# The merge with W_A done inside the gate loop one block behind, the gated convolution kept in SBUF, and the router fed by DMA transposes of the split rows

## The chip, the cores and the metric

The kernel runs on one core of a Trainium2 chip. A time is the device time of one execution in microseconds (us). The kernel before was timed in three runs: 1108.13, 1108.33 and 1110.32 us, so its median is 1108.33 us. A further execution, the profiled one, took 1110.83 us, of which 1109.1 us lie between the first and the last instruction (the span); the other 1.7 us lie around it.

## The reference, cut to what matters

One decoder layer on x of 1024 tokens by 1024 features, all in float32:

```python
h = rms_norm(x, attn_norm_g)
q, k, v, f_logit, cb, cc, cu, ga, gb = split(h @ w_in)
y_att  = forgetting_attention(q, k, v, log_f)              # 1024 x 512
y_conv = cb * causal_short_conv(cc * cu, conv_w)           # 1024 x 512
merged = (sigmoid(ga) * (y_att @ w_out_att)                # W_A
          + sigmoid(gb) * (y_conv @ w_out_conv))           # W_B
x  = x + merged @ w_o
h2 = rms_norm(x, ffn_norm_g)
x  = x + hierarchical_moe(h2, w_rg, b_rg, w_re, b_re, ...) # 4 + 16 router columns
h3 = rms_norm(x, ple_norm_g)
x  = x + sigmoid(h3 @ w_pg) * (p @ w_ple)
```

The change touches the lines from `merged` to the router's logits (h2 @ [w_rg | w_re]).

## The kernel before, in words

**Numbers.** Nearly every large product is made of fp16 pairs. `split` (L108) writes a float32 tile as a high part (ScalarE, L110) and a low part (VectorE, L111); `mm3` (L116 to L119) then does three matmuls for each 128-row piece of the contraction: high by high, high by low, low by high. They add up in a PSUM bank of 128 x 512 float32. There are banks named acc (2), tr (2), s (3) and o (1).

**Stages, in order of time.** (1) Projections and attention, with matmuls of the convolution and of gate_A's logits woven in; the logits go to DRAM (`sga`), the attention result too (`yatt`). (2) The gate loop over eight blocks j of 128 features: for each half of 512 tokens, 24 matmuls of gate_B's logits (`feat_mm`, L542, into acc, weights `wgb`; block 0's are done earlier), a sigmoid on ScalarE (L560), 12 matmuls of y_conv with W_B (tiles bmh and bml, into s, L564) and a product on VectorE (L565). The result `sg` is written to DRAM (`cgb`, L566). (3) The merge loop (`merge_in`, `merge`, L590 to L621): for each block it loads `sga` and `cgb` back, takes the sigmoid, does 12 matmuls for each half with W_A and the attention result (yh, yl, into acc), multiplies on VectorE (L607), adds on GpSimd (L608) and splits the sum into mTh and mTl (L609). The eight pieces of w_o are loaded and split along the way (`wo_in`, L581). (4) out_proj (L652): for each of eight token tiles t and each half h, 24 matmuls of mTh, mTl with w_o, and x added by VectorE (L663). `norm2` (L665) makes the normed rows h2, split into h2s, and writes them to DRAM for the experts. The router of tile t-1 stands between: `x2_t` (L682) transposes the float32 rows on TensorE (L687), `pieces` (L674) cuts them into three bf16 parts on ScalarE, VectorE and GpSimd (L675 to L680), `router_mm` (L691) does 24 matmuls of 60 columns (L700). (5) A window for the last tile whose order is written by hand (L880 on): the last out_proj, the routing, and the first matmuls of the last stage (`ple_mm`, L866). (6) The experts and (7) the last combination.

**What sets the order.** Outside the window a scheduler places the instructions on each engine, from dependences and from tiles coming free; each engine, and each engine's queue of DMA issues, then runs strictly in its order. In the attention part ScalarE and VectorE follow the written order until L559. SyncE (SP) issues the weight loads, L533 (`wpiece`), L569, L584, L595, and the x loads, L629. Pools open and close like a stack; a tile in a space that another tile had waits for the last use there. `wraw` tiles in `cp` and `ep` hold raw float32 weights before the split.

Of the kernel before, what the change touches and what calls it, by code (L numbers as in the profile page):

```python
# [9 lines left out]
F32 = mybir.dt.float32  # L10
# [9 lines left out]
S = 1024  # L20
# [6 lines left out]
C = 176  # L27
EPS = 1e-6
WARM = 64
WOJ = (1, 1, 1, 1, 1, 1, 1, 1)  # L30
WOEP = (1, 4, 7)
EA = 1
WRAW = 10
OVR = 2
NPL = 3
# [27 lines left out]
def trunk_layer(ctx: ExitStack, tc: tile.TileContext, x, wq0, wq, wc, wgb, wga, wA, wB, wo, wr,  # L63
# [5 lines left out]
    def pool(stack, name, bufs=1, **kw):  # L69
        return stack.enter_context(tc.tile_pool(name=name, bufs=bufs, reuse_waits="tile", **kw))  # L70
# [3 lines left out]

    yatt = tc.dram_tile([4, 128, S], F32, name="yatt")
    sga_d = tc.dram_tile([8, 128, S], F32, name="sga")
    cgb_d = tc.dram_tile([8, 128, S], F32, name="cgb")
    h2_d = tc.dram_tile([S, 2 * D], FP16, name="h2d")
    mark_d = tc.dram_tile([1, 1], F32, name="mark")
    pl_d = tc.dram_tile([S, D], F32, name="pld")  # L80
# [52 lines left out]
    def o_bank():  # L133
        return bank("o", 1)
# [390 lines left out]
    cstack = ExitStack()  # L525
    cp = pool(cstack, "conv", side="right")
    pieces = itertools.count()

    def wpiece(src, kn, pl_=None):
        i = next(pieces)  # L530
        pl_, n = (cp, 2) if pl_ is None and i % 2 == 0 else (ep, 2)
        raw = pl_.tile([128, 1024], F32, name="wraw", bufs=2 if pl_ is cp else 1)
        nc.sync.dma_start(raw, src)  # L533
        wh = pl_.tile([128, 1024], FP16, name="wh", bufs=n)
        wl = pl_.tile([128, 1024], FP16, name="wl", bufs=n)
        split(wh, wl, raw, scale=HS)
        return (wh.rearrange("p (k m) -> p k m", k=kn), wl.rearrange("p (k m) -> p k m", k=kn))

    def gt_(n=5):
        return ep.tile([128, S], F32, name="g", bufs=n)  # L540

    def feat_mm(wp, h):  # L542
        acc = acc_bank()
        for k in range(8):
            mm3(acc, wp[0][:, k], wp[1][:, k], hTh[:, k, h * 512:(h + 1) * 512],
                hTl[:, k, h * 512:(h + 1) * 512], k, 8)
        return acc

    wBp = None
    for j in range(8):  # L550
        wb = wpiece(wgb[j], 8) if j else None
        if j % 2 == 0:
            wBp = wpiece(wB[j // 2], 4)
        sg = gt_()
        for h in range(2):
            hs = slice(h * 512, (h + 1) * 512)
            a = feat_mm(wb, h) if j else conv["b", h]
            if j == 0 and h == 1:
                order.close()  # L559
            nc.scalar.activation(sg[:, hs], a, AF.Sigmoid, scale=1.0 / PS)  # L560
            b = bank("s", 3)
            jj = slice((j % 2) * 128, (j % 2 + 1) * 128)
            for k in range(4):
                mm3(b, wBp[0][:, k, jj], wBp[1][:, k, jj], bmh[:, k, hs], bml[:, k, hs], k, 4)  # L564
            nc.vector.scalar_tensor_tensor(sg[:, hs], b, 1.0 / PS, sg[:, hs], op0=ALU.mult, op1=ALU.mult)  # L565
        nc.scalar.dma_start(cgb_d[j], sg)  # L566
    for p in range(4):
        yr = cp.tile([128, 1024], F32, name="wraw", bufs=2)
        nc.sync.dma_start(yr, yatt[p])  # L569
        split(yh[:, p], yl_[:, p], yr, scale=XS)  # L570
    cstack.close()
    hstack.close()

    mstack = ExitStack()
    mp = pool(mstack, "merged")
    mTh = mp.tile([128, 8, S], FP16, name="mTh")
# [1 line left out]
    wp_ = pool(mstack, "wo")  # L578
    wos = []

    def wo_in():  # L581
        k = len(wos)
        raw = wp_.tile([128, D], F32, name="woraw", bufs=1) if k not in WOEP else ep.tile([128, D], F32, name="wraw", bufs=1)
# [6 lines left out]
    def merge_in(j):  # L590
        if j % 2 == 0:
            wAs.append(wpiece(wA[j // 2], 4, ep))
        ga, gb = gt_(), gt_()
        for t, d in ((ga, sga_d), (gb, cgb_d)):
            nc.sync.dma_start(t, d[j])  # L595
        nc.scalar.activation(ga, ga, AF.Sigmoid)
        return ga, gb

    def merge(j, ga, gb):
        wAp = wAs[j // 2]  # L600
        jj = slice((j % 2) * 128, (j % 2 + 1) * 128)
        for h in range(2):
            hs = slice(h * 512, (h + 1) * 512)
            a = acc_bank()
            for k in range(4):
                mm3(a, wAp[0][:, k, jj], wAp[1][:, k, jj], yh[:, k, hs], yl_[:, k, hs], k, 4)
            nc.vector.scalar_tensor_tensor(ga[:, hs], a, 1.0 / PS, ga[:, hs], op0=ALU.mult, op1=ALU.mult)  # L607
            nc.gpsimd.tensor_tensor(ga[:, hs], ga[:, hs], gb[:, hs], op=ALU.add)  # L608
            split(mTh[:, j, hs], mTl[:, j, hs], ga[:, hs], scale=XS)  # L609

    wAs, gs = [], []
    for j in range(EA):
        gs.append(merge_in(j))
    for j in range(8):
        if j + EA < 8:
            gs.append(merge_in(j + EA))
        for _ in range(WOJ[j]):
            wo_in()
        merge(j, *gs[j])
    while len(wos) < 8:  # L620
        wo_in()  # L621
    estack.close()
    ystack.close()

# [40 lines left out]
    def norm2(t):  # L665
        h2 = fp.tile([128, D], F32, name="h2", bufs=1)
        rs = row_norm(fp, x2[:, t], gF, h2)
        hs = fp.tile([128, 2, D], FP16, name="h2s", bufs=2)
        nc.scalar.activation(hs[:, 0], h2, AF.Copy)
        nc.vector.tensor_tensor(hs[:, 1], h2, hs[:, 0], op=ALU.subtract)  # L670
        nc.scalar.dma_start(h2_d[t * 128:(t + 1) * 128, :], hs.rearrange("p a d -> p (a d)"))
        return rs

    def pieces(src, parts, rest, eng, extra):  # L674
        nc.scalar.activation(parts[0], src, AF.Copy)  # L675
# [4 lines left out]
        eng.tensor_tensor(parts[2], rest, parts[1], op=ALU.subtract)  # L680

    def x2_t(t, g, fast=False, extra=None):  # L682
        xT = [fp.tile([128, 512], BF, name=f"x2T{i}", bufs=2) for i in range(3)]
        rest = fp.tile([128, 512], F32, name="rest", bufs=1)
# [163 lines left out]
    tb = bank("s", 3)  # L848
    for t in range(NT - 1):
        out_proj(t, 0)  # L850
        if t:
            xT = [x2_t(t - 1, g) for g in range(2)]
        out_proj(t, 1)
        if t:
            router_mm(t - 1, xT, rs)
        rs = norm2(t)
        if t == 4:
            nc.sync.dma_start(wpl, wple)
            nc.sync.dma_start(pTs[0], pT[:, :, :NPL * 128])
# [31 lines left out]
    tr = tr_bank()
    for c in range(4):
# [523 lines left out]
```

## Time and profile before

| | us |
|---|---|
| median of three runs | 1108.33 |
| the profiled execution | 1110.83 |
| its span | 1109.1 |
| gate loop (first bmh matmul to 574) | 460.8 to 574 |
| merge loop | 574 to 625.2 |
| out_proj with norm and router, tiles 0 to 6 and the first half of 7 | 625.2 to 712 |
| hand-ordered window | 712 to 751 |
| experts and the rest | 751 to 1109 |

Over the span TensorE (PE) is busy 94%, VectorE (DVE) 61%, ScalarE (ACT) 49%, GpSimd (POOL) 23%; the granted TensorE clock is 0.975 of full speed in the mean. The stages can be told apart by their lines: matmuls named `s<-bmh,wh` belong to the gate loop, `acc<-yh,wh` to the merge, `acc<-woh,mTh` to out_proj. A matmul row's start is exact enough for a pitch: matmuls are issued one behind another, and each one's listed duration overlaps with its successor's. So time on PE is counted from start to start.

### The profile page before, as it was taken

To read this page: it belongs to the slowest core of one execution; us is meant where nothing else is said; L and a number is where in the kernel's file an instruction comes from. 1 tells how busy PE (TensorE), PEld (TensorE's weight loads), DVE (VectorE), ACT (ScalarE), POOL (GpSimd) and SP (SyncE) were. 2 spreads that over 40 slices of the span, in tenths; PEclk is the share of its full clock that TensorE was granted. 3 is DMA by queue.
4 is the path that set the end of the run, shared out by engine and by line. 5 is a ranking of instruction groups with operands and counts; after the bars stand their busy time and mean duration, and the time that the engine had idled before them with its cause. 6 is when DMAs were issued, how large, how long until landed. Compare 5 with 4: busy or idle time off the path is not lost. (4 is left out here: it accounts for less than half of the span.)

```text
span 1109.1 us, 18207 instructions
## 1 busy us (share of the span) xinstructions
PE 1042.5 (94%) x6776; PEld 602.0 (54%) x6776; DVE 674.2 (61%) x1441; ACT 538.9 (49%) x1001; POOL 253.1 (23%) x364
## 2 busy tenths in 40 slices
PE   5969999999999999999997999987989999997998
PEld 3634555555555544444443455446757777753454
DVE  4866776676666553222337555764987888855633
ACT  4654555555554552212225334345776777753232
POOL 4653333233322000000014322241211111014300
PEclk8979999999999999999999999988999999999999
DMA  7355778675684752333448531159999999716501
GB/s 237 113 120 139 141 157 181 160 140 138 151 163 116 164 134 79 116 105 123 152 139 285 211 128 57 39 175 364 399 380 333 311 337 316 232 62 229 209 39 57
DMA packets 152543, 197.69 MB, mean 178 GB/s; under 512 B 108162, under 2 KB 111754, under 8 KB 152322
## 3 DMA queue, kind: packets, MB, share of 16 engines
q1 hardware_dynamic: 128194, 117.28, 36.9%
q0 software_dynamic: 15136, 53.42, 15.4%
q10 hardware_dynamic: 9120, 25.78, 6.1%
q8 instruction: 54, 0.88, 0.3%
q14 instruction: 39, 0.32, 0.1%
HBM read 138.69 MB, written 32.59 MB: 154 GB/s over the span
## 5 line engine op out<-in xcount | busy, mean ns | idle before, releaser
L118 PE MATMUL acc<-hTl,fwh 128*128 128x512 f16 x336 | 128.4, 382 | 0.0
L117 PE MATMUL acc<-hTh,fwh 128*128 128x512 f16 x336 | 128.3, 382 | 0.0
L119 PE MATMUL acc<-hTh,fwl 128*128 128x512 f16 x336 | 128.2, 381 | 0.0
L947 DVE SCALAR_TENSOR_TENSOR wl<-wraw,wh 128x1024 f16<-128x1024 f32 x64 | 77.4, 1218 | 21.8 <-ACT wh L942 21.8
L111 DVE SCALAR_TENSOR_TENSOR wl<-wraw,wh 128x1024 f16<-128x1024 f32 x47 | 57.0, 1223 | 54.3 <-ACT wh L110 52.8
L228 PE MATMUL acc<-wqh,hTh 128*128 128x384 f16 (+1 forms) x248 | 82.2, 331 | 6.9 <-ACT hTh L110 3.1
L230 PE MATMUL acc<-wql,hTh 128*128 128x384 f16 (+1 forms) x248 | 81.8, 330 | 1.1 <-DVE wql L111 1.1
L229 PE MATMUL acc<-wqh,hTl 128*128 128x384 f16 (+1 forms) x248 | 81.9, 330 | 0.3 <-DVE hTl L111 0.3
L314 ACT ACTIVATE P<-P,st 128x128 f32<-128x128 f32 (+3 forms) x64 | 49.4, 772 | 60.3 <-DVE st L311 40.1
L110 ACT ACTIVATE wh<-wraw 128x1024 f16<-128x1024 f32 x47 | 49.1, 1054 | 55.9 <-PE acc L118 27.5
L942 ACT ACTIVATE wh<-wraw 128x1024 f16<-128x1024 f32 x64 | 66.8, 1052 | 16.1 <-PE acc L1027 8.5
L306 DVE CUSTOM_DVE_ANT_0 P<-s,base 128x512 f32<-128x512 f32 (+2 forms) x96 | 51.2, 552 | 24.4 <-PE s L305 19.4
L323 DVE SCALAR_TENSOR_TENSOR hl<-P,st,hl 128x128 f16<-128x128 f32 (+3 forms) x64 | 52.9, 841 | 17.3 <-ACT hl L322 17.0
L119 PEld LDWEIGHTS <-fwl 128*128 128x128 f16 x336 | 33.1, 98 | 39.3 <-issue 1.1
L1027 PEld LDWEIGHTS <-wh 128*128 128x128 f16 x512 | 50.5, 99 | 5.3 <-issue 1.7
L322 ACT ACTIVATE hl<-P,st 128x128 f16<-128x128 f32 (+3 forms) x64 | 46.5, 767 | 13.7 <-ACT P L314 8.4
L117 PEld LDWEIGHTS <-fwh 128*128 128x128 f16 x336 | 33.1, 98 | 36.0 <-issue 2.4
L1026 PEld LDWEIGHTS <-wh 128*128 128x128 f16 x512 | 51.1, 100 | 1.8
L1310 PE MATMUL acc<-wh,xl 128*128 128x512 f16 (+1 forms) x136 | 49.9, 367 | 2.3 <-DVE xl L111 2.3
L118 PEld LDWEIGHTS <-fwh 128*128 128x128 f16 x336 | 33.0, 98 | 34.4 <-issue 1.1
L991 POOL DMA_INDIRECT xg<-h2d,toki x16 | 18.1, 1131 | 145.0 <-PE tr L1006 135.7
L1311 PE MATMUL acc<-wl,xh 128*128 128x512 f16 (+1 forms) x136 | 49.9, 367 | 0.0
(323 smaller groups left out, 2642.8 us busy)
## 6 DMA issues: line engine op xcount, KB each, us to landing
wraw<-in_we_dram SPq DMA_DIRECT2D x96, 512.0 KB, 6.9
Yd<-yt ACTq DMA_DIRECT2D x14, 512.0 KB, 7.4
fraw<-in_wc_dram POOLq DMA_DIRECT2D x12, 512.0 KB, 5.2
wraw<-in_wq_dram POOLq DMA_DIRECT2D x24, 192.0 KB, 3.9
P<-in_x_dram SPq DMA_DIRECT2D x8, 512.0 KB, 7.4
fraw<-in_wga_dram POOLq DMA_DIRECT2D x8, 512.0 KB, 4.9
base<-brow POOLq DMA_DIRECT2D x8, 512.0 KB, 4.8
sga<-fg POOLq DMA_DIRECT2D x8, 512.0 KB, 3.1
```

Of the source, the lines that this page charges most:

```text
L111: nc.vector.scalar_tensor_tensor(lo, src, scale, hi, op0=ALU.mult, op1=ALU.subtract)
L117: nc.tensor.matmul(acc, lhsT=whi, rhs=xhi, start=k == 0, stop=False)
L118: nc.tensor.matmul(acc, lhsT=whi, rhs=xlo, start=False, stop=False)
L119: nc.tensor.matmul(acc, lhsT=wlo, rhs=xhi, start=False, stop=k == nk - 1)
L228: nc.tensor.matmul(acc[:, :w], lhsT=hTh[:, k, tok], rhs=wh[:, :w], start=k == 0, stop=False)
L229: nc.tensor.matmul(acc[:, :w], lhsT=hTl[:, k, tok], rhs=wh[:, :w], start=False, stop=False)
L230: nc.tensor.matmul(acc[:, :w], lhsT=hTh[:, k, tok], rhs=wl[:, :w], start=False, stop=k == 7)
L306: nc.vector.tensor_tensor_reduce(out=pt[:, c0:c0 + valid], in0=sb[:, :valid], in1=base[:, c0:c0 + valid], scale=1.0, scalar=-3e38, op0=ALU ...
L323: nc.vector.scalar_tensor_tensor(hl[:, :qt + 1, 1], p3, r, hl[:, :qt + 1, 0], op0=ALU.mult, op1=ALU.subtract)
L942: nc.scalar.activation(wh, raw, AF.Copy, scale=HS)
L947: V_.scalar_tensor_tensor(wl, raw, HS, wh, op0=ALU.mult, op1=ALU.subtract)
L1026: nc.tensor.matmul(a[:, :n], lhsT=wh[:, k], rhs=xT[:, k, 0, :n], start=k == 0, stop=False)
```

## The change

Three things change. First, the merge moves: in round j of one loop over j = 0 to 8 the gate work of block j is done and then the merge of block j-1, into the tr banks. The gated convolution stays in SBUF (`gb`, three buffers), so its eight writes to DRAM and eight reads back are gone; the sum with it is now on VectorE (L590 after) and not on GpSimd. One piece of w_o is loaded and split in each round; `wraw` has three buffers, `wh` and `wl` five. Second, the router of tiles 0 to 6 reads DMA transposes (issued by SP) of the split rows h2s, one transposed tile hT2 of 16 blocks of 128 x 128 for each token tile, and does 8 matmuls of 40 and 8 of 20 columns with a split router weight `wrp`; the last tile keeps the old way. Third, since pools open and close at other places, the tiles hTh, hTl are held until after the window, and the loads of gF, the router weights and pT stand behind the x loads.

```diff
-    cgb_d = tc.dram_tile([8, 128, S], F32, name="cgb")
...
-    for j in range(8):
-        wb = wpiece(wgb[j], 8) if j else None
...
-            nc.vector.scalar_tensor_tensor(sg[:, hs], b, 1.0 / PS, sg[:, hs], op0=ALU.mult, op1=ALU.mult)
-        nc.scalar.dma_start(cgb_d[j], sg)
-    for p in range(4):
-        yr = cp.tile([128, 1024], F32, name="wraw", bufs=2)
-        nc.sync.dma_start(yr, yatt[p])
-        split(yh[:, p], yl_[:, p], yr, scale=XS)
-    cstack.close()
-    hstack.close()
...
+    def half_mm(a, wp, xh, xl, jj, hs):
+        for k in range(4):
+            mm3(a, wp[0][:, k, jj], wp[1][:, k, jj], xh[:, k, hs], xl[:, k, hs], k, 4)
+    gB, wAB = {}, {}
+    for j in range(9):
+        if j < 8:
+            wb = wpiece(wgb[j], 8) if j else None
+            if j % 2 == 0:
+                wAB[j // 2] = [wpiece(wB[j // 2], 4)]
+            sg = gB[j] = ep.tile([128, S], F32, name="gb", bufs=3)
+            for h in range(2):
...
+                nc.scalar.activation(sg[:, hs], a, AF.Sigmoid, scale=1.0 / PS)
+                b = bank("s", 3)
+                half_mm(b, wAB[j // 2][0], bmh, bml, slice((j % 2) * 128, (j % 2 + 1) * 128), hs)
+                nc.vector.scalar_tensor_tensor(sg[:, hs], b, 1.0 / PS, sg[:, hs], op0=ALU.mult, op1=ALU.mult)
+            if j == 0:
+                for p in range(4):
+                    yr = ep.tile([128, 1024], F32, name="wraw", bufs=3)
+                    nc.sync.dma_start(yr, yatt[p])
+                    split(yh[:, p], yl_[:, p], yr, scale=XS)
+            if j % 2 == 0:
+                wAB[j // 2].append(wpiece(wA[j // 2], 4))
             wo_in()
+            ga = ep.tile([128, S], F32, name="ga", bufs=3)
+            nc.sync.dma_start(ga, sga_d[j])
+            nc.scalar.activation(ga, ga, AF.Sigmoid)
+            gB[j] = (gB[j], ga)
+        if j:
+            i = j - 1
+            gb, ga = gB.pop(i)
+            for h in range(2):
+                hs = slice(h * 512, (h + 1) * 512)
+                a = tr_bank()
+                half_mm(a, wAB[i // 2][1], yh, yl_, slice((i % 2) * 128, (i % 2 + 1) * 128), hs)
+                nc.vector.scalar_tensor_tensor(ga[:, hs], a, 1.0 / PS, ga[:, hs], op0=ALU.mult, op1=ALU.mult)
+                nc.vector.tensor_tensor(ga[:, hs], ga[:, hs], gb[:, hs], op=ALU.add)
+                split(mTh[:, i, hs], mTl[:, i, hs], ga[:, hs], scale=XS)
...
+    split(wrp[:, :, 0], wrp[:, :, 1], wrt, scale=HS)
...
-        return rs
+        hT2 = fp.tile([128, 2, 8, 128], FP16, name="hT2", bufs=2)
+        nc.sync.dma_start_transpose(hT2.rearrange("p a k t -> p (a k) t"), hs.rearrange("p a d -> p (a d)"))
+        return hT2
+    def router_rows(t, hT2):
+        rb = o_bank()
+        for k in range(8):
+            nc.tensor.matmul(rb[:, :40], lhsT=hT2[:, 0, k], rhs=wrp[:, k].rearrange("p a e -> p (a e)"), start=k == 0,
+                             stop=False)
+            nc.tensor.matmul(rb[:, :20], lhsT=hT2[:, 1, k], rhs=wrp[:, k, 0], start=False, stop=k == 7)
...
         out_proj(t, 0)
-        if t:
-            xT = [x2_t(t - 1, g) for g in range(2)]
         out_proj(t, 1)
         if t:
-            router_mm(t - 1, xT, rs)
-        rs = norm2(t)
+            router_rows(t - 1, hT2)
+        hT2 = norm2(t)
...
     out_proj(T, 0)
-    xT = [x2_t(T - 1, g) for g in range(2)]
...
-    out_proj(T, 1, lambda: router_mm(T - 1, xT, rs))
+    out_proj(T, 1)
...
+    router_rows(T - 1, hT2)
     router_mm(T, last, ss[:, 3:4])
...
+    hstack.close()
```

The first place is SP's queue from the end of attention on; wgb, wB, wA and wo name the four weights, yatt the attention result. Before:

```order
L324 DMA_TRANSPOSE pTr<-hl 128x16x128
L533 DMA wraw<-in_wB_dram 128x1024
L533 DMA wraw<-in_wgb_dram 128x1024 x3
L533 DMA wraw<-in_wB_dram 128x1024 x2
L533 DMA wraw<-in_wgb_dram 128x1024 x4
L569 DMA wraw<-yatt 128x1024
L533 DMA wraw<-in_wB_dram 128x1024
L569 DMA wraw<-yatt 128x1024 x3
L533 DMA wraw<-in_wA_dram 128x1024 x2
L595 DMA g<-sga 128x1024
L595 DMA g<-cgb 128x1024
```

After:

```order
L530 DMA wraw<-in_wB_dram 128x1024
L573 DMA wraw<-yatt 128x1024 x2
L539 DMA woraw<-in_wo_dram 128x1024
L579 DMA ga<-sga 128x1024 x3
L573 DMA wraw<-yatt 128x1024 x2
L530 DMA wraw<-in_wA_dram 128x1024
L539 DMA woraw<-in_wo_dram 128x1024
L530 DMA wraw<-in_wgb_dram 128x1024 x2
L530 DMA wraw<-in_wB_dram 128x1024
```

The attention result and W_A's first piece, which stood behind all gate weights, now stand ahead of the first two of them.

The second place is VectorE in the merge of one block; g (before) and ga (after) hold the gate and then the sum. Before, in the merge loop:

```order
L607 SCALAR_TENSOR_TENSOR g<-acc,g 128x512
L111 SCALAR_TENSOR_TENSOR mTl<-g,mTh 128x512
L111 SCALAR_TENSOR_TENSOR wol<-woraw,woh 128x1024
L607 SCALAR_TENSOR_TENSOR g<-acc,g 128x512
L111 SCALAR_TENSOR_TENSOR mTl<-g,mTh 128x512
L111 SCALAR_TENSOR_TENSOR wl<-wraw,wh 128x1024
```

After, in the joint loop:

```order
L107 SCALAR_TENSOR_TENSOR wl<-wraw,wh 128x1024
L589 SCALAR_TENSOR_TENSOR ga<-tr,ga 128x512
L590 TENSOR_TENSOR ga<-ga,gb 128x512
L107 SCALAR_TENSOR_TENSOR mTl<-ga,mTh 128x512
L589 SCALAR_TENSOR_TENSOR ga<-tr,ga 128x512
L590 TENSOR_TENSOR ga<-ga,gb 128x512
L107 SCALAR_TENSOR_TENSOR mTl<-ga,mTh 128x512
L569 SCALAR_TENSOR_TENSOR gb<-s,gb 128x512
L107 SCALAR_TENSOR_TENSOR wl<-wraw,wh 128x1024
L569 SCALAR_TENSOR_TENSOR gb<-s,gb 128x512
```

The add has come to VectorE, and the products of the gate loop (L569) stand among those of the merge.

The third place is TensorE in out_proj, where the router's operand is made or used. Before, between the halves of a tile:

```order
L662 LDWEIGHTS mTh
L662 MATMUL acc<-wol,mTh 128x512
L687 MATMUL tr<-identF,x_6012 128x128 x8
L660 LDWEIGHTS mTh
L660 MATMUL acc<-woh,mTh 128x512
```

After, the first router matmuls (hT_6125 is tile 0's hT2):

```order
L634 LDWEIGHTS mTh
L634 MATMUL acc<-wol,mTh 128x512
L651 LDWEIGHTS hT_6125
L651 MATMUL o<-wrp,hT_6125 128x40
L653 LDWEIGHTS hT_6125
L653 MATMUL o<-wrp,hT_6125 128x20
L651 LDWEIGHTS hT_6125
```

The transposes are gone from TensorE. Tile 0's router stands 99 matmuls of out_proj behind tile 0's own last one; those of tiles 1 to 5 stand 72, 59, 60, 59 and 72 behind theirs, and tile 6's stands in the window behind the last tile's transposes.

The fourth place is SP behind the merge, where hT2's transposes are issued. Before, the loads of gF, wrt and part of pT stood in the row behind the first place; after:

```order
L599 DMA x_5982<-in_x_dram 128x1024 x8
L610 DMA gF<-in_gains_dram 128x1024
L616 DMA wrt<-in_wr_dram 128x160
```

They stand behind the eight x loads now, and wple, pT and the seven transposes (L645) follow them.

## Rows read from the trace of the kernel before

**Rows 1.** Windows by stage: busy us of each engine (count), clock, DMA share, GB/s.

```profile
461.00:574.00 113.00, 113.00 (x525) 51.22 (x524) 29.94 (x32) 25.51 (x32) 1.51 (x11) 1.00 0.39 133
574.00:625.00 51.00, 44.76 (x196) 19.36 (x194) 39.42 (x48) 25.44 (x31) 21.20 (x15) 0.97 0.70 237
625.00:712.00 87.00, 87.00 (x566) 44.94 (x565) 50.52 (x117) 32.68 (x64) 19.88 (x21) 1.00 0.27 105
712.00:724.00 12.00, 9.66 (x67) 5.02 (x64) 9.18 (x38) 4.12 (x9) 3.54 (x3) 0.86 0.11 45
...
751.00:1006.00 255.00, 235.25 (x2364) 179.09 (x2362) 194.15 (x309) 172.27 (x251) 36.57 (x62) 0.99 0.85 299
```

**Rows 2.** Waits of TensorE, 440 to 760: total us, times, longest.

```profile
PE acc L117 <- DVE g L607: 6.2, 6, 2.2
...
PE s L117 <- ACT wh L110: 1.6, 1, 1.6
```

**Rows 3.** Timeline of TensorE, four starts: start us, us, engine, line.

```profile
460.78 0.39 PE L117 MATMUL s<-bmh,wh 128*128 128x512 f16 x1 [1.63 <-ACT wh L110]
...
533.31 0.38 PE L117 MATMUL s<-bmh,wh 128*128 128x512 f16 x1
...
564.39 0.38 PE L117 MATMUL s<-bmh,wh 128*128 128x512 f16 x1
...
625.24 0.38 PE L660 MATMUL acc<-woh,mTh 128*128 128x512 f16 x1
```

**Rows 4.** Timeline of GpSimd and of VectorE in the merge loop.

```profile
582.31 1.79 POOL L608 TENSOR_TENSOR g<-g 128x512 f32<-128x512 f32 x1 [2.67 <-DVE g L607]
...
582.94 2.25 DVE L111 SCALAR_TENSOR_TENSOR wol<-wraw,woh 128x1024 f16<-128x1024 f32 x1
585.11 0.68 DVE L607 SCALAR_TENSOR_TENSOR g<-acc,g 128x512 f32<-128x512 f32 x1
...
591.64 1.23 DVE L111 SCALAR_TENSOR_TENSOR wl<-wraw,wh 128x1024 f16<-128x1024 f32 x1 [1.57 <-ACT wh L110]
```

**Rows 5.** Groups of TensorE by shape, 440 to 760: busy us, mean ns, idle.

```profile
L700 PE MATMUL o<-wrb,x2T 128*128 128x60 bf16 x180 | 9.4, 193 | 0.0
L687 PE MATMUL tr<-identF,x 128*128 128x128 f32 x60 | 7.9, 274 | 2.3 <-DVE rest L676 2.3
```

**Rows 6.** Timeline of TensorE in out_proj and in the window.

```profile
640.78 1.04 PE L687 MATMUL tr<-identF,x 128*128 128x128 f32 x8
641.65 0.38 PE L660 MATMUL acc<-woh,mTh 128*128 128x512 f16 x1
...
715.92 0.66 PE L687 MATMUL tr<-identF,x 128*128 128x128 f32 x4 [2.34 <-DVE rest L676]
...
720.04 0.38 PE L660 MATMUL acc<-woh,mTh 128*128 128x512 f16 x1
...
721.45 0.77 PE L700 MATMUL o<-wrb,x2T 128*128 128x60 bf16 x22
722.06 0.38 PE L660 MATMUL acc<-woh,mTh 128*128 128x512 f16 x1
```

**Rows 7.** Timeline, norm of token tile 0: from x's second half to h2s.

```profile
635.80 0.69 DVE L663 SCALAR_TENSOR_TENSOR x<-acc,x 128x512 f32<-128x512 f32 x1 [3.62 <-PE acc L662]
...
641.98 0.33 ACTq L671 DMA_DIRECT2D h2d<-h2s  x1
```

**Rows 8.** Line L324, the DMA transposes of attention: landing.

```profile
DMA to landing us min/median/max: 2.3/3.8/4.8
```

**Rows 9.** Line L252, the transposes of the projections: landing.

```profile
DMA to landing us min/median/max: 2.7/2.8/6.0
```

**Rows 10.** Line L629, the x loads: issues and landing.

```profile
L629 SPq DMA_DIRECT2D x<-in_x_dram x8: 333/435/557, 627.5 to 630.9; - x8
...
DMA to landing us min/median/max: 3.6/6.8/11.1
```

**Rows 11.** Line L569, the loads of the attention result: landing.

```profile
DMA to landing us min/median/max: 3.3/3.3/3.4
```

More of the change, by code (lines that the diff above doesn't have):

```diff
@@ L29 @@
 WARM = 64
-WOJ = (1, 1, 1, 1, 1, 1, 1, 1)
-WOEP = (1, 4, 7)
-EA = 1
 WRAW = 10
@@ L524, in trunk_layer @@
     ep = pool(estack, "ep", side="right")
[L525 to L549, printed above, removed]
-    for j in range(8):
-        wb = wpiece(wgb[j], 8) if j else None
[L552 to L564, printed above, removed]
-            nc.vector.scalar_tensor_tensor(sg[:, hs], b, 1.0 / PS, sg[:, hs], op0=ALU.mult, op1=ALU.mult)
-        nc.scalar.dma_start(cgb_d[j], sg)
-    for p in range(4):
-        yr = cp.tile([128, 1024], F32, name="wraw", bufs=2)
-        nc.sync.dma_start(yr, yatt[p])
-        split(yh[:, p], yl_[:, p], yr, scale=XS)
-    cstack.close()
-    hstack.close()
     mstack = ExitStack()
@@ L579, in trunk_layer, with wpiece @@
     wos = []
+    def wpiece(src, kn):
+        raw = ep.tile([128, 1024], F32, name="wraw", bufs=3)
+        nc.sync.dma_start(raw, src)
+        wh = ep.tile([128, 1024], FP16, name="wh", bufs=5)
+        wl = ep.tile([128, 1024], FP16, name="wl", bufs=5)
+        split(wh, wl, raw, scale=HS)
+        return (wh.rearrange("p (k m) -> p k m", k=kn), wl.rearrange("p (k m) -> p k m", k=kn))
     def wo_in():
         k = len(wos)
-        raw = wp_.tile([128, D], F32, name="woraw", bufs=1) if k not in WOEP else ep.tile([128, D], F32, name="wraw", bufs=1)
+        raw = wp_.tile([128, D], F32, name="woraw", bufs=1)
         nc.sync.dma_start(raw, wo[:, k, :])
@@ L588, in wo_in @@
         wos.append((wh, wl))
[L590 to L617, printed above, removed]
-            wo_in()
-        merge(j, *gs[j])
-    while len(wos) < 8:
-        wo_in()
+    def half_mm(a, wp, xh, xl, jj, hs):
[11 more added lines that the diff above has]
+                if j:
+                    a = acc_bank()
+                    for k in range(8):
+                        mm3(a, wb[0][:, k], wb[1][:, k], hTh[:, k, hs], hTl[:, k, hs], k, 8)
+                else:
+                    a = conv["b", h]
+                if j == 0 and h == 1:
+                    order.close()
+                nc.scalar.activation(sg[:, hs], a, AF.Sigmoid, scale=1.0 / PS)
[9 more added lines that the diff above has]
+                wAB[j // 2].append(wpiece(wA[j // 2], 4))
+            wo_in()
+            ga = ep.tile([128, S], F32, name="ga", bufs=3)
+            nc.sync.dma_start(ga, sga_d[j])
+            nc.scalar.activation(ga, ga, AF.Sigmoid)
+            gB[j] = (gB[j], ga)
+        if j:
+            i = j - 1
+            gb, ga = gB.pop(i)
+            for h in range(2):
+                hs = slice(h * 512, (h + 1) * 512)
+                a = tr_bank()
[3 more added lines that the diff above has]
+                split(mTh[:, i, hs], mTl[:, i, hs], ga[:, hs], scale=XS)
@@ L644, in trunk_layer @@
     wrb = fp.tile([128, 8, 60], BF, name="wrb")
+    wrp = fp.tile([128, 8, 2, 20], FP16, name="wrp")
     nc.sync.dma_start(wrt, wr)
+    split(wrp[:, :, 0], wrp[:, :, 1], wrt, scale=HS)
     nc.vector.tensor_tensor(wrt, wrt, vt[:, 40:48, None].to_broadcast([128, 8, 20]), op=ALU.mult)
@@ L671, in norm2 @@
         nc.scalar.dma_start(h2_d[t * 128:(t + 1) * 128, :], hs.rearrange("p a d -> p (a d)"))
-        return rs
+        hT2 = fp.tile([128, 2, 8, 128], FP16, name="hT2", bufs=2)
[3 more added lines that the diff above has]
+        rb = o_bank()
+        for k in range(8):
+            nc.tensor.matmul(rb[:, :40], lhsT=hT2[:, 0, k], rhs=wrp[:, k].rearrange("p a e -> p (a e)"), start=k == 0,
+                             stop=False)
+            nc.tensor.matmul(rb[:, :20], lhsT=hT2[:, 1, k], rhs=wrp[:, k, 0], start=False, stop=k == 7)
+        sm = fp.tile([128, 20], F32, name="sm", bufs=2)
+        nc.vector.tensor_reduce(sm, rb[:, :40].rearrange("p (w e) -> p e w", e=20), axis=AX.X, op=ALU.add)
+        nc.vector.scalar_tensor_tensor(lg[:, t], sm, 1.0 / PS, vt[:, 14:34], op0=ALU.mult, op1=ALU.add)
     def pieces(src, parts, rest, eng, extra):
@@ L682, in x2_t @@
     def x2_t(t, g, fast=False, extra=None):
-        xT = [fp.tile([128, 512], BF, name=f"x2T{i}", bufs=2) for i in range(3)]
-        rest = fp.tile([128, 512], F32, name="rest", bufs=1)
+        xT = [fp.tile([128, 512], BF, name=f"x2T{i}", bufs=1) for i in range(3)]
+        rest = fp.tile([128, 1024], F32, name="hT2", bufs=2)[:, :512]
         tr = tr_bank()
```

## The prediction

> **What bounds the kernel now.** I read the windows by stage first: TensorE is busy all 113 us of the gate loop and all 87 us of out_proj at full granted clock, while VectorE is busy 30 and 51 us there [rows 1]. In the merge loop it is busy 44.8 of 51 us, and there VectorE (39.4 us) and the DMA engines (share 0.70) are loaded most [rows 1]. So TensorE's own instruction stream sets the time, but for the places where it waits. The waits of TensorE between 440 and 760 us name them: 6.2 us, in six pieces, on the product of the merge (VectorE L607), which must free an acc bank, and 1.6 us at the start of the gate loop [rows 2]; the groups by shape give 2.3 us before the router's transposes [rows 5]. I then put a price on the streams, from start to start on the timeline. Between 533.31 and 564.39 us lie two gate blocks without a wait, 144 matmuls in 31.08 us, so 0.2158 us each [rows 3]. From the first bmh matmul, 460.78, to the first of out_proj, 625.24, are 164.46 us [rows 3]; the stream there holds 336 gate_B matmuls (blocks 1 to 7), 192 with W_B and 192 with W_A, 720 x 0.2158 = 155.4 us. 9.1 us are in excess: the 6.2 us of waits, and 2.9 us in which PE ran at half clock (0.97 in the merge window, 1.5 us of 51 [rows 1]) or refilled.
>
> Why VectorE was late: the low part of a w_o piece took 2.25 us with GpSimd's add beside it, and a weight of the same size 1.23 us without [rows 4]. The add itself took 1.79 us, and the next wait stands behind it.
>
> **The change part by part.**
>
> *Gate and merge.* The 720 matmuls remain. In the joint loop a round has 48 + 24 + 24 = 96 matmuls, 20.7 us. VectorE's work in a round: two products of the gate loop, two of the merge and two low parts, of 0.68 us like the old merge's row of that shape [rows 4]; three low parts of weights (wgb, w_o, and half of wB and of wA each) at 1.23 us [rows 4]; two adds that the trace doesn't show on VectorE. GpSimd's 1.79 us [rows 4] bounds one above, zero below; 0.7 us is taken, the 1.23 us row being for twice the elements. That makes 6 x 0.68 + 3 x 1.23 + 1.4 = 9.2 us (11.4 with 1.79) in 20.7, where in the merge loop it was 39.4 of 51. GpSimd has no add left, so the 2.25 us row should go back to 1.23. The merge has the tr banks to itself, so the acc banks wait for ScalarE's sigmoid only. Of the 6.2 us of waits I expect nothing to stay, of the other 2.9 us 1.5. Term: 9.1 - 1.5 = -7.6 us; bounds: 0 (all turns into other waits) and -9.1. The 16 transfers of 512 KB that go were hidden and are worth nothing by themselves.
>
> *Start of the joint loop, an added wait.* TensorE does the 48 bmh matmuls of blocks 0 and 1 first (10.4 us, to 471.1), then the merge of block 0, which needs the attention result and W_A's first piece. These loads stand behind three `sga` loads on SP and wait for a `wraw` tile, so for a split. A load of this kind landed in 3.3 us [rows 11], its low part takes 1.23 [rows 4], and two such turns pass: they end about at 471. The matmuls of gate block 1 are queued behind. Cost 0 to 3.3 (one turn more); taken 0.5, as two turns fit.
>
> *out_proj.* A tile before cost 48 x 0.2158 = 10.36, 8 transposes at (641.65 - 640.78)/8 = 0.109 us, and 24 router matmuls at (722.06 - 721.45)/22 = 0.028 us [rows 6]: 11.9 us. Of the 60 transposes [rows 5] 56 go: -6.1 us. Of the 180 router matmuls [rows 5] 168 go and 112 come; a new one has the same weight load of 128 x 128 and fewer columns, so 0.028 is taken for it (0.02 to 0.04 as ends): -4.7 + 3.1 = -1.6 us (-2.5 to -0.2). The piece-making on ScalarE, VectorE and GpSimd goes too, but they were not what ended last, so that is worth nothing but slack.
>
> *The transposed operand, an added wait at each tile.* Behind out_proj(t,1)'s end come the add to x, the norm and the split: 641.98 - 635.80 = 6.2 us [rows 7]; then SP issues the transpose. The old trace has no transpose of h2s, but attention's largest ones, 16 blocks of 128 x 128 fp16 as well, are among those that landed in 2.3 to 4.8 us [rows 8], and other ones took up to 6.0 [rows 9]. I take 4.8: 6.2 + 4.8 and half a microsecond of hand-over make 11.5 us. The router's 16 matmuls stand at least 59 matmuls of out_proj behind, 12.7 us. Slack 1.2 us; queued behind the waiting matmul is the whole of out_proj, so any lack is paid in full by the end. With 6.0 the lack is 0 too. Taken 0.3 us in all; ends 0 and 7.7 (1.1 us in each tile).
>
> *x, gF.* The x loads wait for the end of the merge, as before; they were issued from 627.5 to 630.9, the last landing up to 11.1 us later, so 14.5 us after the first issue [rows 10]. The first add needs x one transfer (3.6 us) after: 0.3 us taken, up to 2. gF comes behind these eight loads now, and VectorE's scaling of gF stands in its order ahead of the norm and of the last add of tile 1. If M is the last merge matmul, x is issued at M + 3.5, gF lands at about M + 19, and the add of tile 1 ends at M + 22.7. TensorE wants that bank after 36 + 48 + 24 matmuls, M + 23.3. Margin 0.6 us; taken 0.4, up to 4 with a slower landing.
>
> *Window.* The stall of 2.3 us before the transposes [rows 5] goes with them. After it TensorE ran at half clock: from 715.92 to 720.04 it did 4 transposes and 10 matmuls, 4.12 us for 4 x 0.109 + 10 x 0.2158 = 2.59, so 1.5 us lost [rows 6]; the window's 0.86 says the same [rows 1]. What is late next is the add to x before the last transposes, which was late before. Of 3.8 us I take -3.0; ends -3.8 and 0. The experts behind start from this window and have TensorE busy 235 of 255 us [rows 1]; they are taken to shift as a whole.
>
> *Sum.* -7.6 - 6.1 - 1.6 - 3.0 + 0.5 + 0.3 + 0.3 + 0.4 = -16.8 us. The durations are of the profiled execution, 1110.83 us, so it would be 1094.0; that execution was 2.5 us above the median of the runs, and on the median 1108.33 it is 1091.5 us.
>
> **A rule that speaks against it.** The largest transposes of this size landed in at most 4.8 us [rows 8]. The Trainium skill, "VectorE: DVE Perf Modes", sections "The three transpose paths" and "Rules for kernel authors", advises TensorE for a 128 x 128 transpose where PSUM will do as a target, and prices the DMA crossbar at 1309 ns against 390 ns. Sixteen blocks one after another would by that page make an estimated 20.9 us, the router would come some 15 us late in each tile, and the time would go to about 1195 us. The trace disagrees with such a serial sum, with its 4.8 us for 16 blocks.
>
> **The rivals.**
> A. The operand is a little late in every tile: transposes share the DMA engines with 4 MB of x, gF, wple and pT at the beginning, and TensorE loses 1.1 us in each of 7 tiles. For it: the slack is only 1.2 us. Against: out_proj's DMA share was 0.27 [rows 1]. 1091.5 + 7.7 = 1099.2 us. Chance 0.11.
> B. The joint loop starves: SP's order puts the first two pieces of wgb behind eleven other transfers, and each load waits for a `wraw` tile. For it: the merge loop had a DMA share of 0.70 [rows 1]. Against: the round of 20.7 us now moves some 2 MB, 100 GB/s, and the old gate loop moved 133 with no wait. The merge's gain is lost: 1091.5 + 7.6 = 1099.1. Chance 0.06.
> C. Slower: the transposes of h2s land much later than attention's. TensorE's orders are strict, so each microsecond beyond 12.7 - 6.7 = 6.0 us is paid in each of 7 tiles. The point from which it decides is 16.8 / 7 = 2.4 us above this, a landing of 8.4 us; with 10 us the time is 1091.5 + 7 x 4.0 = 1119.5. The rule above is of this kind. For it: the longest transposes seen, 4.8 and 6.0 us, came under light traffic, and SP has other loads queued ahead. Against: none reached 8.4 [rows 8, 9]. Chance 0.05.
> D. The time before the experts is not TensorE's: routing of the last tile, and the experts' loads (DMA share 0.85 [rows 1]) set the end, and what is won above is waited for in the window. 1106 to 1109 us. Against: the last tile's routing begins from TensorE's last out_proj, and the experts' first loads stand on SP behind the last tile's rows, so both begin earlier with it. Chance 0.05.
> E. All terms at their better ends: -9.1 - 6.1 - 2.5 - 3.8 = -21.5, about 1087. Chance 0.03.
>
> **How the numbers follow.** My forecast, 1091.5 us, has 0.70, with its own range 1087.5 to 1095.5 from the ends of the waits and of the window. The range that should hold 8 in 10 takes in E, A and B: 1086.5 to 1099.5. A measurement of this kernel tells about 0.2%, 2.2 us, from no change. Faster by more: forecast, A, B and E, 0.90. Within: D but for a fifth of it, 0.04. Slower: C and that fifth, 0.06.
>
> **What would show it.** In the new trace: from the first bmh matmul to the last of the merge about 157 us instead of 164.5, no wait of TensorE on a product of the merge, no w_o low part above 1.3 us; at the 471st microsecond a pause of under 1 us; a tile of out_proj every 10.8 us instead of 11.9, no weight load of hT2 that waits, and one that landed in 4 to 5 us; no half-clock row about the last tile. The first expert matmul comes some 17 us earlier. The forecast is wrong if TensorE waits for hT2 or gF for more than 3 us in all, if the joint loop has waits for weights, or if the expert stage is longer than before by what was won.

## The result, and the profile after

The changed kernel took 1095.32 us in the median of four runs (1092.79 to 1097.78) against 1108.95 us for the kernel before, measured with it: a ratio of 0.9876, 95% interval 0.985 to 0.9902, so 13.7 us or 1.2% less. Run again later it gave 1092.47 against 1112.94 us for before beside it, 0.9821 (0.9795 to 0.9846). The forecast of 1091.5 us and its range, 1086.5 to 1099.5, hold; the first measurement lies 3.8 us above the forecast.

The profiled execution took 1095.96 us with a span of 1094.2: 14.9 us less than before's span. The windows by stage of the changed kernel, cut at the events of the table below and without the experts (columns as in [rows 1]):

```profile
459.50:618.00 158.50, 158.18 (x732) 71.37 (x733) 71.78 (x88) 51.84 (x64) 1.52 (x11) 1.00 0.31 102
618.00:706.50 88.50, 85.67 (x490) 40.46 (x488) 49.27 (x140) 22.04 (x45) 5.24 (x8) 0.98 0.58 162
706.50:731.00 24.50, 21.13 (x109) 11.27 (x110) 18.76 (x82) 11.26 (x19) 11.21 (x11) 0.93 0.68 227
987.70:1094.20 106.50, 98.00 (x480) 49.91 (x480) 50.30 (x80) 30.84 (x67) 24.17 (x26) 0.95 0.36 129
```

In the first row TensorE (PE) is busy 158.2 of 158.5 us; in [rows 1] the merge part had 44.8 of 51. In the last row the clock is 0.95.

Its waits of TensorE, 440 to 760 us, beside [rows 2]:

```profile
PE tr L989 <- DMA xtail<-h2d,toki: 3.3, 1, 3.3
PE tr L989 <- ACT xT L994: 2.3, 1, 2.3
PE o L651 <- DMA hT<-h2s: 2.1, 1, 2.1
PE s L742 <- DVE oh L740: 2.0, 4, 1.4
PE s L113 <- ACT wh L106: 1.6, 1, 1.6
PE tr L874 <- DVE x L635: 0.7, 1, 0.7
PE o L684 <- DVE sm L655: 0.7, 1, 0.7
PE tr L989 <- DMA xg<-h2d,toki: 0.5, 1, 0.5
...
PE tr L115 <- DVE wl L107: 0.2, 1, 0.2
```

Two rows of the same list for the kernel before, which [rows 2] leaves out:

```profile
PE tr L893 <- DVE x L663: 3.0, 1, 3.0
...
PE s L758 <- DVE oh L756: 0.4, 2, 0.2
```

The 6.2 us on the merge's product are gone, and up to the merge's end only 0.2 us on a weight's low part (L115) have come in their place. New are 2.1 us on the transposed tile (L651); the wait on VectorE's routing (L742, before L758) has grown from 0.4 to 2.0 us; the wait on the add to x ahead of the last transposes (L874, before L893) has fallen from 3.0 to 0.7 us. The first two rows, 3.3 and 2.3 us, stand in the experts, of which this window holds 29 us here and 9.5 us before.

For every kernel I cut the span at five events on TensorE: first bmh matmul; end of the merge (the 12 out_proj matmuls that the new order puts ahead of that end are counted to the next leg); first transpose of the last half tile; first expert matmul; first transposes of the last stage. Here are the cuts of the changed kernel, from its timeline; [rows 3] has two of those of before, and its others are at 727.71, 750.50 and 1007.02 us.

```profile
459.52 0.39 PE L113 MATMUL s<-bmh,wh 128*128 128x512 f16 x1 [1.63 <-ACT wh L106]
...
618.17 0.38 PE L632 MATMUL acc<-woh,mTh 128*128 128x512 f16 x1
...
706.50 0.66 PE L874 MATMUL tr<-identF,x 128*128 128x128 f32 x4 [0.74 <-DVE x L635]
...
730.98 0.24 PE L1009 MATMUL acc<-xT,wh 128*128 128x176 f16 x1
...
987.69 1.49 PE L152 MATMUL tr<-identF,x 128*128 128x128 f32 x8 [3.04 <-DVEq L1218]
```

| leg, us | before | changed | again | merge alone | router alone |
|---|---|---|---|---|---|
| gate and merge | 164.5 | 156.1 | 156.8 | 156.7 | 162.5 |
| out_proj, router | 102.5 | 90.9 | 89.4 | 102.5 | 88.5 |
| window to first expert | 22.8 | 24.5 | 25.3 | 23.2 | 25.2 |
| experts | 256.5 | 256.7 | 255.5 | 259.5 | 255.4 |
| last stage | 102.1 | 106.5 | 104.5 | 102.4 | 101.7 |

So -8.4 and -11.5 us were won, 1.7 given back in the window and 4.4 in the last stage; the first bmh matmul, behind code that is the same, came 1.3 us earlier by itself. The sum is the 14.9 us of the span.

Where most of the 4.4 us went shows on the timeline of TensorE in the last stage of the changed kernel:

```profile
1016.18 0.38 PE L1292 MATMUL acc<-wh,xh 128*128 128x512 f16 x1
1020.44 0.61 PE L1293 MATMUL acc<-wh,xl 128*128 128x512 f16 x1 [3.88 <-DVE xl L107]
1020.84 0.63 PE L1294 MATMUL acc<-wl,xh 128*128 128x512 f16 x1
1021.26 0.63 PE L1292 MATMUL acc<-wh,xh 128*128 128x512 f16 x1
```

Behind a wait of 3.9 us the matmuls run 0.43 us from start to start, half the clock, until 1025.7: 13 of them, 2.6 us lost. In the kernel before the wait is 1.6 us shorter and the clock stays:

```profile
1037.99 0.39 PE L1310 MATMUL acc<-wh,xl 128*128 128x512 f16 x1 [2.27 <-DVE xl L111]
1038.22 0.38 PE L1311 MATMUL acc<-wl,xh 128*128 128x512 f16 x1
```

### The profile page after: what moved, and what is told of

Its sections match the earlier page's. It is cut to its first block, busy times and chain, and to the rows that moved or that the text cites. A ratio compares the mean times of both kernels' runs of the same rounds, so it can differ in the third digit from the quotient of the medians.

```text
span 1094.2 us, 17874 instructions
## 1 busy us (share of the span) xinstructions
PE 1035.9 (95%) x6664; PEld 596.5 (55%) x6664; DVE 667.3 (61%) x1444; ACT 525.4 (48%) x974; POOL 213.7 (20%) x334
## 5 line engine op out<-in xcount | busy, mean ns | idle before, releaser
L115 PE MATMUL acc<-hTh,fwl 128*128 128x512 f16 x336 | 127.3, 379 | 0.0
L302 DVE CUSTOM_DVE_ANT_0 P<-s,base 128x512 f32<-128x512 f32 (+2 forms) x96 | 51.3, 553 | 24.5 <-PE s L301 19.3
L319 DVE SCALAR_TENSOR_TENSOR hl<-P,st,hl 128x128 f16<-128x128 f32 (+3 forms) x64 | 53.0, 842 | 16.8 <-ACT hl L318 16.5
L115 PEld LDWEIGHTS <-fwl 128*128 128x128 f16 x336 | 32.9, 98 | 38.7
L1292 PE MATMUL acc<-wh,xh 128*128 128x512 f16 (+1 forms) x136 | 50.9, 374 | 0.0
```

The costliest lines, as they stand in the source:

```text
L1292: nc.tensor.matmul(a, lhsT=xh[:, k], rhs=wh[:, hs], start=k == 0, stop=False)
```

## The experiments

All but e4 (one round) were timed in five rounds; ratios are to the kernel before on the same chip.

**a0, the changed kernel again**, with no edit.

> The changed kernel once more, for its spread and its clock. Theory: its executions differ only by half-clock stretches of TensorE, so span times granted clock is about 1066.5 us in each (1091.1 x 0.978, 1092.9 x 0.976, 1094.2 x 0.975 gave 1067.1, 1066.7, 1066.8), and the time lies between 1092 and 1098 us, ratio 0.985 to 0.990. In this profile the wait before the last stage's matmuls (low part of x, 3.9 us in the first profile) need not be followed by ten matmuls at half clock. Rival: the give-back in the last stage is part of the change, then every profile has it: 4 to 5 us more than before from the first expert matmul to the end.

Measured: 1092.47 us (1089.59 to 1094.41), ratio as above, lower than expected; span times clock 1063.9 to 1069.7, not as constant as I wrote. The last stage had the wait (3.1 us) and the half clock once more (104.5 us). Of the 14 profiles, the last stage took 101.7 to 102.7 us in before, e1, e2, e4, e5, e7 and e10, and 104.0 to 106.6 in the changed kernel and a0, e3, e6, e8, e9, e11. So a longer last stage goes with most versions that have both parts, but not with all. The rival as written does not hold: from the first expert matmul to the end a0 took 360.0 us and before 358.6, 1.4 us more and not 4 to 5; the first profile took 363.2, e10 353.9, and e1 and e7, with one part or none, 361.9 and 361.2. The wait in the last stage was 1.6 to 2.8 us in the former group and 2.3 to 3.9 in the latter, so the wait alone does not decide it. What does is open.

**e1, the merge alone.**

```diff
-            router_rows(t - 1, hT2)
-        hT2 = norm2(t)
+            router_mm(t - 1, xT, rs)      # with x2_t between the halves, as before
+        rs = norm2(t)
```

> Only the joint loop; the router as before. Theory: the loop's gain (excess 9.1 us before, 0.7 in the changed kernel) stands alone: 8.4 us less, about 1100.5 us, and the window keeps its 2.3 us wait before the router's transposes and the half-clock piece behind it. Rival: the loop's gain depends on the router part (out_proj bound elsewhere): less than 3 us, 1106 or more.

Measured: 1105.42 us, 0.9948 (0.9929 to 0.9966), 5.8 us, less than the 8.4 expected, which lie outside the interval; the rival's 3 us are outside it too. The first leg is 156.7 us, 7.8 less than before, as the theory has it; the 2.3 us wait before the router's transposes (2.4) and a half-clock piece behind it are still there. The experts' leg was 2.9 us longer in this profile, and over the 14 profiles it lies between 251.9 and 259.5 us, so a few us of a gain can be hidden there.

**e2, the router alone**: the loops of before, with norm2, router_rows and the window of the change.

> Only the router by DMA transposes; gate and merge loops as before. Theory: from the first out_proj matmul to the transposes of the last half tile 11.5 us were won, 1.7 given back behind it: about 10 us less, 1099 us; the merge's waits of 6.2 us stay. Rival: the two parts overlap, and this one alone is worth less than 6 us, 1103 or more.

Measured: 1099.66 us, 0.9898 (0.9872 to 0.9924), 11.3 us. Two rows of its waits:

```profile
PE acc L117 <- DVE g L607: 5.8, 7, 1.2
PE s L117 <- ACT wh L110: 1.6, 1, 1.6
```

The merge's waits stay at 5.8 us. The parts add, as far as the noise tells: 5.8 + 11.3 = 17.1 us, and 19.9 for the whole on the same chip in the same rounds, each of the three with an error of 2 to 3 us. The old loops took 162.5 us here, 2 less than before's own profile, whose merge had a piece at half clock; so some 2 of the 8.4 us depend on the execution.

**e3, the write of the rows behind the transpose.**

```diff
-        nc.scalar.dma_start(h2_d[t * 128:(t + 1) * 128, :], ...)   # ahead of the transpose
+        nc.sync.dma_start(h2_d[t * 128:(t + 1) * 128, :], ...)     # behind it
```

> The changed kernel with the write of the normed rows to DRAM issued behind their transpose, on SP, and not beside it on ScalarE's queue. In the changed kernel the transposed tile came 6.3 to 6.6 us after its issue (640.90 to 647.15, 691.32 to 697.92) where attention's took 4.8 at most. Theory: the write of the same rows at the same moment takes the DMA engines; with it behind, the tile comes in at most 5.2 us, the wait of 2.1 us for tile 5's operand falls under 0.8, and the time falls by 1 to 3.5 us against the changed kernel. Rival: the transposes of 16 blocks of this layout take 6.3 us by themselves; nothing changes, within 1 us.

Measured: 1092.11 us, 0.9821, the same as a0. The line of the transposes, first of e2 (write beside it), then of e3:

```profile
L675 SPq DMA_TRANSPOSE hT<-h2s x7: 1687/3958/4391, 642.9 to 709.6; - x7
...
DMA to landing us min/median/max: 5.6/6.0/6.4
```

```profile
L644 SPq DMA_TRANSPOSE hT<-h2s x7: 1317/1935/2892, 643.2 to 700.0; - x7
...
DMA to landing us min/median/max: 4.3/4.7/4.9
```

With the write behind it the transpose of 16 blocks lands in 4.7 us, near the longest of attention's [rows 8]; beside a 512 KB write of the same rows in 6.0. The edit moves the write to another queue as well as behind, so that the two share the DMA engines is the likely reason and not shown by itself. TensorE's wait on the tile fell from 2.1 to 0.3 us and out_proj's leg to 87.9 us, 1.5 to 3 less. The window's grew to 26.0, and the time did not move: the write's effect on the landing is shown, the expected gain in time is not.

**e4, each transpose twice into the same tile.**

> The changed kernel with each DMA transpose issued twice into the same tile, the second behind the first, so that the operand comes about 12 us after the first issue and not about 6. TensorE's order places the router some 15 matmuls (3 us) later. Theory: the operand is on TensorE's path, the distance is about 16 us and 6.7 + 12 are needed: 2 to 3 us lost in each of seven tiles, 1105 to 1115 us, and waits of TensorE on the transposed tile of 12 us or more in all. Rival: the operand has slack enough; within 4 us of the changed kernel.

Measured: 1104.77 us, 0.9931 (0.9912 to 0.995), just under the range given, some 12 us more than a0 by the ratios. TensorE waited 7.4 us in five pieces, not 12:

```profile
PE o L652 <- DMA hT<-h2s: 7.4, 5, 2.3
```

The out_proj leg grew to 98.0 us, and the wait on the last add to x is back at 3.0 us. The operand is on TensorE's path, but TensorE waits less for it than I gave.

**e5, the split rows transposed by TensorE.**

```diff
-        nc.sync.dma_start_transpose(hT2..., hs...)
+        for a in range(2):
+            tr = tr_bank().bitcast(FP16)
+            for c in range(8):
+                nc.tensor.transpose(tr[:, c * 128:(c + 1) * 128], hs[:, a, c * 128:(c + 1) * 128], identH)
+            # copied out by ScalarE (a = 0) and VectorE (a = 1)
```

> The changed kernel with the same split rows transposed by TensorE (16 fp16 transposes of 128 x 128 in a token tile, 0.056 us each by the rows of the experts' transposes) and copied out of PSUM by ScalarE and VectorE. Theory: 7 x 16 x 0.056 = 6.2 us more on TensorE, minus the 2 us wait and 1 us of half clock that the DMA way has: 2 to 5 us slower than the changed kernel. Rival, the rule that prefers TensorE for 128 x 128 blocks: not slower, since no operand comes late any more.

Measured: 1100.23 us, 0.99 (0.9875 to 0.9925), some 8.8 us more than a0 by the ratios; I had expected 2 to 5. Its timeline of TensorE:

```profile
643.25 1.06 PE L651 MATMUL tr<-identH,h2s 128*128 128x128 f16 x16
644.14 0.38 PE L632 MATMUL acc<-woh,mTh 128*128 128x512 f16 x1
...
706.03 0.61 PE L651 MATMUL tr<-identH,h2s 128*128 128x128 f16 x8 [2.03 <-DVE hT L671]
```

16 transposes take 0.89 us, 6.2 in seven tiles, as expected; the wait for the operand is not gone but has become one of 2.0 us for a PSUM bank (VectorE's copy is late), and eight matmuls at half clock follow it. So here, on the kernel's busiest engine and with the copies out of PSUM that the router's operand needs, transposing on TensorE costs time, and 16 blocks by DMA landed in 4.7 us (e3). The Trainium skill ("VectorE: DVE Perf Modes", "Rules for kernel authors") advises TensorE for a 128 x 128 block where PSUM will do as a target; the 20.9 us estimated from the page's 1309 ns did not come.

**e6, the add back on GpSimd in the joint loop** (`nc.vector.tensor_tensor` to `nc.gpsimd.tensor_tensor`, L590).

> The changed kernel with the merge's add on GpSimd as before. Theory: the gain of the joint loop comes from spreading the merge's VectorE work over 20.7 us of matmuls; low parts of weights beside an add stretch to about 2.3 us, but the leg from the first bmh matmul to the end of the merge stays at 156 to 158 us and the time within 1.5 us of the changed kernel. Rival: the gain comes from taking GpSimd off; the leg grows by more than 3 us.

Measured: 1093.56 us, 0.9842 (0.9819 to 0.9866). A low part beside an add took up to 2.34 us again, and the first leg stayed at 156 us. So GpSimd's share costs nothing in this loop, where a round has room.

**e7, the kernel before with its add on VectorE** (the opposite edit, L608).

> The kernel before with nothing changed but the merge's add, now on VectorE. Theory: VectorE alone is what the merge loop waits for; it gains back the stretched low parts and pays 16 adds of 0.7 us, so its waits stay between 3 and 8 us and the time within 3 us of before. Rival: GpSimd's share was the cause; the waits of 6.2 us go and the time falls by 5 us or more.

Measured: 1112.86 us, 1.0021 (1.0001 to 1.0042). The window over its merge loop (columns as in [rows 1]):

```profile
574.00:625.00 51.00, 46.19 (x211) 20.39 (x210) 43.85 (x66) 26.51 (x33) 0.00 (x0) 1.00 0.71 237
```

VectorE's low parts of weights all took 1.2 us, but it is busy 43.9 of 51 us [rows 1 has 39.4], and TensorE still waits 4.8 us, in six pieces, on the product. The first leg is 161.3 us, 1.2 less than e2's and 3.2 less than before's, of which the time shows nothing. The old merge loop had too little matmul time for its VectorE work, and taking GpSimd off does not mend that. One thing no run separates: the joint loop also put the merge into the tr banks, and whether more banks alone would have hidden the waits of the old loop is not shown.

**e8, the round trip through DRAM kept.**

```diff
+            nc.scalar.dma_start(cgb_d[j], sg)
+            gc = ep.tile([128, S], F32, name="gc", bufs=2)
+            nc.sync.dma_start(gc, cgb_d[j])
-            gB[j] = (gB[j], ga)
+            gB[j] = (gc, ga)
```

> The changed kernel with the gated convolution still written to DRAM and read back (8 writes and 8 reads of 512 KB, as before), the merge using what was read. Theory: these transfers were hidden and still are, a round of 20.7 us stands between; the leg from the first bmh matmul to the end of the merge stays at 156 to 157.5 us, the time within 2 us of the changed kernel. Rival: keeping it in SBUF is where the gain is; the leg grows by 3 us or more.

Measured: 1094.94 us, 0.9832 (0.9807 to 0.9857); first leg 155.8 us. The 16 transfers are hidden, as the theory has it.

**e9, the transposes in halves**, the high parts ahead of the low parts' subtraction.

> The changed kernel with the operand transposed in two halves: the high parts as soon as ScalarE has them, the low parts later. Theory: the second half has half the data and lands some 1 to 2 us earlier than the whole (6.0 to 6.6 us after issue), TensorE's wait on it falls from 2 us to under 1; out_proj's leg 1 to 2 us shorter than 89.4 to 90.9. Rival: each transpose has a cost of its own and shares the engines with the write; the operand comes no earlier, and the leg stays.

Measured: 1094.03 us, 0.9836 (0.9806 to 0.9865). The high half landed in 3.1 us, the low half in 4.7 to 6.0, issued 1.4 us later: hardly earlier than the whole. The wait fell to 1.0 us, the leg to 88.3; in the time nothing shows.

**e10, tile 6's router in a bank of its own, with e3's write.**

> The kernel with the write behind the transpose, and besides tile 6's router result in an acc bank and not in the only o bank, which the last tile's router waits for (0.7 us on VectorE's sm). Theory: part of what the window gives back (25 to 26 us from the last transposes to the first expert matmul, 22.8 before) is this wait; it goes, and the window's leg falls by 0.5 to 0.8 us. Rival: the next wait (VectorE's routing work, 1.3 us on oh) takes its place: leg as before, 25.5 to 26.

Measured: 1091.69 us, 0.9819 (0.9794 to 0.9843). The wait of 0.7 us is gone, yet the window's leg is 26.7 us. Its timeline of TensorE shows what is late next:

```profile
729.08 0.40 PE L989 MATMUL tr<-identH,xg 128*128 128x128 f16 x4 [1.47 <-DMA xg<-h2d,toki]
730.18 0.57 PE L989 MATMUL tr<-identH,xtail 128*128 128x128 f16 x4 [0.70 <-DMA xtail<-h2d,toki]
...
734.74 0.24 PE L1009 MATMUL acc<-xT,wh 128*128 128x176 f16 x1
```

The first gathered rows of the experts come 1.5 us after TensorE is ready, and half clock follows. In before TensorE was not ready ahead of them there. The gather, which follows the routing, was issued at 721.07, so its rows came 8.0 us later; in e3 they came within 6.4 us. Why it took longer is open. So the time won on TensorE in the window was waited away at the gather in this run; the rival is right, with another wait than it named.

**e11, the routing's first piece one tile earlier** (`CUTS = (0, 3, 6, NT)`).

> The changed kernel with the first piece of routing over tiles 0 to 2 instead of 0 to 3, and the second over 3 to 5. Theory: tile 5's operand was late (wait 1.5 to 2.1 us) because VectorE did the first piece's routing ahead of tile 5's split rows; with the piece a tile earlier, tile 5's wait falls under 0.5 us, and another tile (4, or 6) may wait instead, under 1 us. Rival: tile 5 is late for the transposes' landing alone (6.6 us); the wait stays at 1.5 us or more.

Measured: 1093.89 us, 0.9833 (0.981 to 0.9857). TensorE no longer waits for any transposed tile, so VectorE's routing work was what made tile 5 late; a wait of 1.8 us on the add to x ahead of the first transposes of the last tile (L671) takes its place, longer than the microsecond that I allowed. No gain in time.

No version differs from the changed kernel by more than its interval for the better.

## Why the prediction was right, step by step

*Gate and merge, -7.6 us.* Measured -8.4 (of the 9.1 us in excess 0.7 are left), -7.8 in e1; against e2, whose old loops ran at full clock, it is 6.4. The mechanism holds: VectorE's adds took 0.69 us as assumed (0.7), no low part of w_o more than 1.226 us, no wait on a product. Its cause is the room in a round (with the banks, as said under e7), not GpSimd's absence (e6, e7), and the DRAM traffic was worth nothing (e8). *The start's wait, 0.5:* 0.2 us on wl (0.8 and 0.2 in a0). *x and gF, 0.7:* no wait; gF's scaling began 18.4 us behind the last merge matmul, 636.39 us, where 19 was reckoned, and the bank was free in time.

*out_proj, operand and window, -10.4 together (-6.1, -1.6, -3.0, +0.3).* Measured by the two legs, -11.5 and +1.7, -9.9 us, and -10.6 in a0. The tile's pitch fell as computed: the routers of tiles 2, 3 and 4 start at 660.20, 671.17 and 681.89, 11.0 and 10.7 us apart (10.8 forecast), and 16 router matmuls take 0.40 us (0.45). Two of the terms were mis-sized, the operand as too cheap and the window as worth too little, and they cancel in part.

The operand: I took a landing of 4.8 us from attention's row and "ends 0 and 7.7". It was 5.6 to 6.4 in e2 and 6.6 for tile 5 here, since the write of the same rows starts with it (e2, e3). Six of the seven tiles hid it: 59 matmuls and more stood between. Tile 5 did not. These rows of the changed kernel, of VectorE, SP and TensorE, are its chain:

```profile
690.03 1.22 DVE L642 TENSOR_TENSOR h2s<-h,h2s 128x1024 f16<-128x1024 f32 x1
...
691.32 4.61 SPq L645 DMA_TRANSPOSE hT<-h2s  x1
...
697.94 0.19 PE L651 MATMUL o<-wrp,hT 128*128 128x40 f16 x1 [2.10 <-DMA hT<-h2s]
```

VectorE had done the routing's first piece ahead of tile 5's rows (e11), the tile came 6.6 us after its issue, and half clock came behind the wait at 699.3 us, 1.5 us lost. That makes some 3.6 us where the sum had 0.3. Rival A named this kind of loss and gave 1.1 us in each tile; it came in one.

The window: the stall of 2.3 us [rows 5] is gone, and the 1.5 us of half clock behind it too. A third gain was not in the sum. I had said that the add to x before the last transposes is late next, and that the piece-making that goes is worth "nothing but slack". Before, TensorE waited 3.0 us for that add, which stood on VectorE behind the routing's second piece and the last tile's own pieces (L676, L680); now it is done before the routing ends, and the wait is 0.7 us. These are VectorE's rows, before and after:

```profile
724.52 0.68 DVE L676 TENSOR_TENSOR rest<-tr,x2T 128x512 f32<-128x512 f32 x1
...
725.95 0.69 DVE L680 TENSOR_TENSOR x2T<-rest,x2T 128x512 bf16<-128x512 f32 x1
...
726.97 0.68 DVE L663 SCALAR_TENSOR_TENSOR x<-acc,x 128x512 f32<-128x512 f32 x1
```

```profile
705.76 0.69 DVE L635 SCALAR_TENSOR_TENSOR x<-acc,x 128x512 f32<-128x512 f32 x1 [1.44 <-PE s L788]
```

The wait is 3.0 us in e1 and e7, which keep the old router, and 0.7 in e2, so these 2.3 us belong to the router's part. The price stands behind it: tile 5's logits come later, so the rest of the routing's second piece now follows the last transposes, and TensorE waits for it there:

```profile
708.95 0.37 PE L742 MATMUL s<-oh,oh 128*128 128x32 f16 x2 [1.40 <-DVE oh L740]
```

That (2.0 us in four pieces), 0.65 us for the o bank and 0.5 us for the first gathered rows make first expert matmul minus last transposes 24.5 us for 22.8, though less of it runs at half clock (the eight float32 matmuls behind the last router took 5.15 us, 6.68 before). Where the sum had -3.0 the window gave some -4.4: -2.3, -1.5 and -2.3, and 1.7 back.

*What no step had:* the longer last stage, 4.4 us in the first profile, 2.6 of them half clock and 1.6 a longer wait. Without it the span would have fallen by 19.3 us; with it by 14.9, for a forecast of 16.8. The mean of the two measurements of the whole, 13.7 and 19.9, is 16.8 as well, which with errors of 3 us each and with two mis-sized terms that cancel is luck in part. Three signs of the prediction failed: TensorE did wait for a transposed tile (2.1 us, within the 3 us allowed), the tile landed in more than 5 us, and half-clock rows stand about the last tile, behind tile 5's wait and behind the waits for the routing. Rivals B, C and D did not come: no load starved the loop, no transpose landed later than 6.6 us where 8.4 would have decided, and the experts started 19.5 us earlier.

## What to carry to other kernels

Where a short loop waits for another engine and a long loop beside it has room, join them one step apart: the gain here was the room, and neither the engine that did the small work nor the buffer's way through DRAM mattered. A wait for a transfer is reckoned with what is issued at the same moment, not from like transfers elsewhere. Work that is taken off a second engine can bring forward what stands behind it there, so ask what that engine does next before it is put at nothing. And what is won on the busiest engine can be given back at the next thing that it waits for from others, here the routing and the gather, so look one stage on.

## What the runs showed of the hardware

A 512 KB write issued with a DMA transpose of the same rows at the same moment, on another queue, went with a landing of the transpose in 5.6 to 6.4 us instead of 4.3 to 4.9 with the write behind it (e2, e3), and with an issue on SP of 4.0 us instead of 1.9. Executions of the same kernel on one chip spread by up to 9 us (before, beside a0: 1107.5 to 1116.9), with the granted clock between 0.972 and 0.977; the span times the clock spreads by 3.7 us only, so stretches at half clock make much of it. In the profiles such stretches stand behind waits of some 1.5 to 4 us, at places that change, and the same wait of 2.27 us came with one (the last stage of e11) and without one (that of before).
